# Twelve tiles as 512-column products, and twelve taps of four convolution tiles by ScalarE

## The chip, the cores and the metric

The kernel runs on one core of one Trainium2 chip. The metric is the device time of one execution in microseconds (us). An engine here is one of TensorE (PE; its weight loads are listed as PEld), VectorE (DVE), ScalarE (ACT), GpSimd (POOL) and SyncE (SP). POOL and SP issue transfers (DMA) on queues of their own.

## The reference

One layer of a decoder trunk on 256 rows of width 1024, everything in float32:

```
n = rmsnorm(x);  z = n @ w_in            # one projection, cut into parts
c_a, c_g, q, k, v, qi, ki, wi, gc, ga = split(z)
u = c_a * sigmoid(c_g)                   # convolution branch
u = causal depthwise conv, 31 taps per channel, + bias
y_conv = silu(layernorm(u)) @ w_conv_out
score = sum_h wi_h * relu(qi_h . ki)     # index: 8 heads of 64
y_attn = attention of q, k, v over the 64 best-scored keys @ w_attn_out
h = x + (sigmoid(gc) * y_conv + sigmoid(ga) * y_attn) @ w_mix_out
h = h + cross_attention(rmsnorm(h), rmsnorm(mem))
h = h + relu(rmsnorm(h) @ w_ff1)^2 @ w_ff2
out = rmsnorm(h)
```

The convolution is `u'[t] = bias + sum over s of w[30 - s] * u[t - s]`, s = 0 to 30, for each of the 1024 channels. Channels lie on partitions, so there are eight tiles of 128 channels by 256 rows, and a tap is one multiply-add with a scalar per partition.

## The kernel before

Each float32 product is made of three products of a cheaper form: a number is split into a high part (rounded to fp32r) and a low part (the rest), and high x high, high x low and low x high are added in PSUM. A weight chunk of 1 MB comes by one DMA. For each half of it ACT writes the high part (line 312), and DVE the low part (line 315). PE then makes one product tile of 128 columns of the weight by 256 rows, with eight steps of 128 over the width.

A product tile has two forms (`tile_b`, line 407). The **narrow** form takes 24 matmuls of 256 columns: three for each step (`mm3`). The **wide** form takes the high and the low part of the input side by side as 512 columns, so one matmul of 512 columns makes high x high into the left half of the bank and high x low into the right half; eight more matmuls of 256 columns add low x high to the right half. The two halves are added afterwards: `merge` (line 473) copies the right half out with ACT, and DVE adds the left half. `is_wide` (line 439) names the chunks in the wide form. `back` turns the order of the two kinds of matmul around in every second wide tile.

The chunks follow one list (`STREAM`, line 34): conv 0 to 3, index queries qi, index key ki, conv 4 to 7, the two gates gc and ga, v, then q and k in turns, cross-attention keys and values xk and xv, attention-out ao, conv-out co, mix, and so on to the two feed-forward products f1 and f2. A conv chunk `i` (`conv_in`, line 673) gives two product tiles, gate and value; ACT takes the sigmoid of the gate, DVE multiplies, and the result is `u` for conv tile `i`.

Engines take their instructions in the order in which the program writes them. Between product tiles `tick` (line 369) writes a *turn*: one step of each open chain (generators: memory norm, index scores, gates, attention heads, layer norm), then taps. The taps are what fills DVE: every conv tile has a queue of closures (`tap`, line 628), and `fill_one` (line 378) takes one as long as a running estimate of DVE's time lies behind one of PE's by 1000 ns.

Some taps go another way. Conv tiles 2 to 7 form pairs 1, 2 and 3. From time to time (list `added`, line 352, 25 entries with pauses in estimated PE time) `add_tap` (line 649) lets ACT multiply one shift of both tiles of a pair into a buffer `products`, and POOL issues a DMA that adds it to `acc` in place (line 659). The DVE queue of such a pair is held back until its last DMA has had time (`held_back`). The shifts that go this way are 25 down to 1, in the order of `added`. DVE so has 30 taps for tiles 0 and 1, 25 for 2 and 3, 23 for 4 and 5, 17 for 6 and 7.

When a tile has its last tap, its sum goes into `usum`; with the eighth tile the layer norm starts (`layer_norm`, line 811). It needs the mean (`ps_mub`), the variance (`ps_vr`, `ps_rsb`), and waits until all attention heads are through before it applies the result; its output is the input of conv-out. It gives one step a turn. The heads (line 854) also give one step a turn; the last makes the product `ps_o` and splits it at once.

Of the kernel before, what the change touches and what calls it, by code (L numbers as in the profile page):

```python
# [16 lines left out]
P = 128  # L17
D = 1024
S = 256
# [36 lines left out]
N_CHUNK = KT * S  # L56
HALVES = 6
EARLY = (3,)
WHOLE = (("conv", 0),)
SEVEN = tuple(range(1, 14))  # L60
JOINED = 14
# [57 lines left out]
def block_kernel(ctx, tc, x, xt, mem, memt, wst, wki, vecs, convw, gout, out):  # L119
# [30 lines left out]
    def ps_mm(name):  # L150
        return bank("mm", 2, name)
# [194 lines left out]
        return [w if kt is None else w.rearrange("p (k n) -> p k n", k=kt) for w in prepared.pop(key)]  # L346


    chains, fill, turn, done = [], [], [0], []


    added = [(1, 5000)] * 5 + [(2, 5000)] * 2 + [(2, 2500), (3, 3000)] * 5 + [(3, 5000)] * 8 + []
    add_next, ready, held_back = [0.0], {}, []

    def add_some():
# [13 lines left out]
    def tick():  # L369
        for c in list(chains):  # L370
            if next(c, "end") == "end":
                chains.remove(c)
        while (len(fill) > 1 or (fill and (len(done) > 5 or nused[0] < 5))) and dve.total < pe.total - 1000:
            fill_one()
        dve.total = max(dve.total, pe.total - 2000)
        add_some()

    def fill_one():

        some = [q for q in fill[:3] if q is not turn[0]] or fill  # L380
        q = some[0] if len(some[0]) < 10 and len(fill) > 3 else max(some, key=len)
        turn[0] = q
        q.pop(0)()
        if not q:
            fill.remove(q)
# [5 lines left out]
    def start(gen):  # L391
        chains.append(gen)
        return gen

    def split(hi, lo, src):
        act(hi, src, AF.Copy)
        dve.tensor_tensor(out=lo, in0=src, in1=hi.bitcast(F32), op=ALU.subtract)
# [40 lines left out]

    def is_wide(kind, ct):

        return kind in ("f1", "gc", "ga", "ao", "xk", "q", "k") or (kind in ("mix", "co") and ct < 6)

    def form_b(kind, i, x2, after, ps_of=ps_mm):

# [46 lines left out]
    def copy_to(dst):  # L491
        return lambda ct, ps: copy_out(dst[:, ct, :], ps)
# [135 lines left out]
    def tap(t, s):  # L628
        def go():
            j = TAPS - 1 - s  # L630
            if s == 0:
                act(acc[:, t, :], u[:, t, :], AF.Identity, scale=cw[:, t, j : j + 1], bias=cvb[:, t : t + 1])
            else:
                dve.scalar_tensor_tensor(out=acc[:, t, s:], in0=u[:, t, : S - s], scalar=cw[:, t, j : j + 1],
                                         in1=acc[:, t, s:], op0=ALU.mult, op1=ALU.add)
            if s == TAPS - 1:
                done.append(t)
                if len(done) == KT:
                    norms.append(start(layer_norm()))
                if len(done) > 1:  # L640
                    dve.tensor_tensor(out=usum, in0=usum if len(done) > 2 else acc[:, done[0], :],
                                            in1=acc[:, t, :], op=ALU.add)
        return go

    queues, delays, products = {}, {}, []
    for n, (p, _) in enumerate(added):
        delays.setdefault(p, []).append(len(added) - n)

    def add_tap(pair, s):
        if not products:  # L650
# [10 lines left out]
    def conv_tile(i, half):  # L661
        key = ("conv", i)
        w = weights("conv", i, half, KT) if key not in WHOLE else None
        split_ahead()
        ps = ps_mm(f"ps_conv{i}{half}")
        if w:
            tile_b(ps, w, n2)
        else:
            for kt in range(KT):
                pe.matmul(ps[:, :S], whole[key][:, half * KT + kt, :], n_f[:, kt, :], start=kt == 0, stop=kt == KT - 1)  # L670
        return ps

    def conv_in(i):
        psg = conv_tile(i, 0)
        sg = w2(f"sg{i}", F32, (P, S))
        act(sg, psg[:, :S], AF.Sigmoid)
        tick()
        psa = conv_tile(i, 1)
        dve.tensor_tensor(out=u[:, i, :], in0=psa[:, :S], in1=sg, op=ALU.mult)
        tick()  # L680
        tap(i, 0)()
        queue = [tap(i, s) for s in range(1, TAPS) if s not in delays.get(i // 2, ())]
        if i // 2 not in delays:
            fill.append(queue)
        else:
            queues.setdefault(i // 2, []).append(queue)
            if i % 2:
                delay = iter(delays[i // 2])
                ready[i // 2] = lambda: add_tap(i // 2, next(delay))
        if ("conv", i) in WHOLE:  # L690
            load()
# [6 lines left out]

    qi_t = t8("qi_t", F32, (P, 4, S))
    for i in range(2):  # L700
        form_b("qi", i, n2, copy_to(qi_t))
    wk = weights("ki", 0, 0, KT)
    split_ahead()
    ps = ps_mm("ps_ki")
# [62 lines left out]
    start(index_scores())  # L767
    for i in range(4, 8):
        conv_in(i)


    gc_t, ga_t = t8("gc_t"), t8("ga_t")
# [38 lines left out]
    def layer_norm():  # L811
        u2.append(parts_t8("u_p"))
        mub = ps_aux("ps_mub")[:, :S]
        pe.matmul(mub, onesd, usum, start=True, stop=True)
        mub = mub.unsqueeze(1).to_broadcast([P, 2, S])
        vs = w2("vs", F32, (P, 2, S))
        pairs = [slice(2 * c, 2 * c + 2) for c in range(4)]
        for c, cs in enumerate(pairs):
            dve.tensor_tensor(out=acc[:, cs, :], in0=acc[:, cs, :], in1=mub, op=ALU.subtract)
            sq = vs if c == 0 else w2(f"sq_vr{c}", F32, (P, 2, S))  # L820
            act(sq, acc[:, cs, :], AF.Square)
            if c > 1:
                dve.tensor_tensor(out=vs, in0=vs, in1=before, op=ALU.add)
            before = sq
        yield
        dve.tensor_tensor(out=vs, in0=vs, in1=before, op=ALU.add)
        dve.tensor_tensor(out=vs[:, 0, :], in0=vs[:, 0, :], in1=vs[:, 1, :], op=ALU.add)
        yield
        yield
        rs = rsqrt(vs[:, 0, :], "vr")  # L830
        yield
        while len(headed) < NH:
            yield
        act(table, table, AF.Silu)
        rsb = spread(rs, "rsb").unsqueeze(1).to_broadcast([P, 2, S])
        for c in range(5):
            if c < 4:
                dve.tensor_tensor(out=acc[:, pairs[c], :], in0=acc[:, pairs[c], :], in1=rsb, op=ALU.mult)
                for t in (2 * c, 2 * c + 1):
                    act(acc[:, t, :], acc[:, t, :], AF.Silu, scale=lng[:, t : t + 1], bias=lnb[:, t : t + 1])  # L840
                act(u2[0].high(2 * c, 2), acc[:, pairs[c], :], AF.Copy)
            if c > 0:
                parts_of(2 * c - 2)
            yield
# [9 lines left out]
    def head(h, q, k):  # L854
        yield
        yield
        ps = ps_acc(f"ps_s{h}")
        pe.matmul(ps[:, 0:P], q[:, 0:P], k[:, 0:P], start=True, stop=True)
        pe.matmul(ps[:, P : 3 * P], q[:, P:S], k, start=True, stop=True)
        t = w2(f"att_t{h}", F32, (P, 3 * P))  # L860
        yield
        mx = small.tile([P, 2], F32, tag="mx", name=f"mx{h}")
        sm = small.tile([P, 2], F32, tag="sm", name=f"sm{h}")
        for qb in range(2):
            dve.tensor_tensor_reduce(out=t[:, parts[qb]], in0=ps[:, parts[qb]], in1=bias[qb], scale=1.0,
                                     scalar=-3.0e38, op0=ALU.add, op1=ALU.max, accum_out=mx[:, qb : qb + 1])
        dve.tensor_scalar(mx, mx, -ATT_SCALE, None, ALU.mult)
        yield
        p = w2(f"att_p{h}", F32, (P, 3 * P))
        for qb in range(2):  # L870
            act(p[:, parts[qb]], t[:, parts[qb]], AF.Exp, bias=mx[:, qb : qb + 1], scale=ATT_SCALE,
                accum_out=sm[:, qb : qb + 1])
        yield
        dve.reciprocal(sm, sm)
        yield
        for qb in range(2):
            act(p[:, parts[qb]], p[:, parts[qb]], AF.Copy, scale=sm[:, qb : qb + 1])
        yield
        pt = ps_aux(f"ps_pt{h}")
        for j in range(3):  # L880
            pe.transpose(pt[:, j * P : j * P + P], p[:, j * P : j * P + P], ident)
        ptr = w2(f"ptr{h}", F32, (P, 3 * P))
        act(ptr, pt[:, : 3 * P], AF.Copy)
        yield
        po = ps_aux(f"ps_o{h}")
        hs = slice(h * HD, h * HD + HD)
        pe.matmul(po[:, 0:P], v_rm[:, 0, hs], ptr[:, 0:P], start=True, stop=True)
        pe.matmul(po[:, P:S], v_rm[:, 0, hs], ptr[:, P : 2 * P], start=True, stop=False)
        pe.matmul(po[:, P:S], v_rm[:, 1, hs], ptr[:, 2 * P : 3 * P], start=False, stop=True)
        split(o2.high(h), o2.low(h), po[:, :S])  # L890
        headed.append(h)

# [31 lines left out]
    for i in range(4):  # L924
        form_b("ao", i, o2, lambda ct, ps: start(gate_branch(ct, ps)), ps_turn)
    assert not added and not held_back
    while fill:
        fill_one()
    finish(norms[0])
# [626 lines left out]
```

## Time and profile before

| | us |
|---|---|
| median of 3 runs | 498.96 |
| lowest, highest | 498.74, 499.46 |
| profiled execution | 499.24 |
| its span | 497.5 |
| DVE taps in `acc` (x190), busy | 78.1 |
| ACT products of `add_tap` (x50), busy | 21.9 |
| ACT high parts (x133), busy | 138.6 |
| DVE low parts (x133), busy | 161.2 |

The span is that of the instructions in one profiled execution. Busy times of instructions that overlap on an engine count the overlap in each, so the distance between two starts tells more of what one costs than its own duration. The name of a tile stands without its number: `ps_conv` is any conv product tile. Line 84 is the line of the helper through which all PE and DVE instructions pass.

### The profile page before, as it was taken

How to read it: one execution, taken by the hardware profiler on the slowest of the kernel's cores; microseconds unless marked ns; L12 is line 12 of the kernel's file. 1: busy time of each engine (PE TensorE's matmuls, PEld its weight loads, DVE VectorE, ACT ScalarE, POOL GpSimd, SP SyncE). 2: the span in 40 equal slices, each digit the busy share in tenths (PEclk: the TensorE clock that was granted, in tenths of full speed). 3: DMA queues.
4: the chain of work that ended last, by engine and by line, in shares of the span. 5: the costliest groups of instructions: out<-in, count | busy, mean ns of one | idle time of the engine just before them, and what ended most of it. 6: DMA issues, size and time to landing. Idle time of an engine off the chain costs nothing.

```text
span 497.5 us, 8036 instructions
## 1 busy us (share of the span) xinstructions
PE 488.3 (98%) x2976; PEld 436.0 (88%) x2976; DVE 462.4 (93%) x847; ACT 358.3 (72%) x615; POOL 47.2 (9%) x64
## 2 busy tenths in 40 slices
PE   7999999999999999999999999999999999999995
PEld 5999998888888898888889999988998888888884
DVE  5999899999899889999988987899999999999986
ACT  7657787787756667667946658687777878888852
POOL 2002212111112100000000000000010101130000
PEclk9999999999999999999999999999999999999998
DMA  8958678989788753444644552766979878999802
GB/s 317 377 198 263 187 188 256 244 236 263 233 232 241 200 155 119 164 170 169 243 180 170 195 206 108 267 199 143 250 261 299 244 242 265 270 342 322 260 3 85
DMA packets 31848, 108.99 MB, mean 219 GB/s; under 512 B 11056, under 2 KB 11824, under 8 KB 22848
## 3 DMA queue, kind: packets, MB, share of 16 engines
q1 hardware_dynamic: 24416, 93.03, 54.2%
q0 software_dynamic: 7104, 15.24, 15.6%
q8 instruction: 23, 0.38, 0.3%
q10 hardware_dynamic: 288, 0.20, 0.1%
q14 instruction: 17, 0.14, 0.1%
HBM read 99.29 MB, written 1.05 MB: 202 GB/s over the span
## 4 chain that ended last, share of the span: by engine, by line
PE 92%; DVE 3%; DMA 3%; ACT 1%; issue 0%; POOL 0%; DVEq 0%; SPq 0%; POOLq 0%
PE ps_f L84 16%; PE ps_p L84 13%; PE ps_conv L84 10%; PE ps_co L84 5%; PE ps_mix L84 5%; PE ps_ao L84 5%; PE ps_k L84 4%; PE ps_gc L84 4%; PE ps_ga L84 4%; PE ps_q L84 4%; PE ps_v L84 4%; PE ps_xo L84 3%; PE ps_qi L84 2%; PE ps_xq L84 2%; PE ps_xk L84 2%; PE ps_xv L84 2%
## 5 line engine op out<-in xcount | busy, mean ns | idle before, releaser
L84 DVE TENSOR_TENSOR lo<-raw,hi 128x1024 fp32r<-128x1024 f32 x133 | 161.2, 1215 | 2.5 <-ACT hi L312 2.2
L312 ACT ACTIVATE hi<-raw 128x1024 fp32r<-128x1024 f32 x133 | 138.6, 1048 | 4.6 <-DMA raw<-in_wst_dram 4.5
L84 DVE SCALAR_TENSOR_TENSOR acc<-u,cw,acc 128x234 f32<-128x234 f32 (+29 forms) x190 | 78.1, 463 | 1.5 <-DMA acc<-products 1.2
L84 PE MATMUL ps_f<-ff_p,hi 128*128 128x512 f32 (+1 forms) x320 | 72.5, 348 | 0.1
L84 PEld LDWEIGHTS ps_f<-ff_p,hi 128*128 128x128 f32 x320 | 56.2, 189 | 8.5 <-ACT ft L1268 0.5
L84 PE MATMUL ps_f<-ff_p,lo 128*128 128x256 f32 x256 | 46.8, 282 | 0.0
L84 PE MATMUL ps_conv<-n_p,hi 128*128 128x256 f32 x224 | 41.0, 285 | 0.0
L84 PEld LDWEIGHTS ps_f<-ff_p,lo 128*128 128x128 f32 x256 | 39.3, 190 | 1.8
L84 PEld LDWEIGHTS ps_conv<-n_p,hi 128*128 128x128 f32 x224 | 34.8, 190 | 0.8 <-issue 0.7
L659 POOL DMA_DIRECT2D acc<-products x25 | 21.7, 867 | 125.5 <-ACT products L658 41.3
L84 PE MATMUL ps_conv<-n_p,lo 128*128 128x256 f32 x112 | 31.7, 283 | 0.0
L658 ACT ACTIVATE products<-u,cw 128x231 f32<-128x231 f32 (+24 forms) x50 | 21.9, 489 | 0.0
L84 PEld LDWEIGHTS ps_conv<-n_p,lo 128*128 128x128 f32 x112 | 21.3, 190 | 0.0
L290 ACT ACTIVATE inner<-sums 128x1024 fp32r<-128x1024 f32 x13 | 13.8, 1060 | 10.4 <-DVE sums L84 10.4
L84 DVE TENSOR_TENSOR ft<-ft 128x128 f32<-128x128 f32 (+2 forms) x49 | 19.4, 396 | 1.2 <-ACT ft L1268 0.7
L84 PE MATMUL ps_p<-outer,fs 128*128 128x512 f32 x78 | 20.1, 393 | 0.0
L84 PE MATMUL ps_v<-hi,n_p 128*128 128x512 f32 x64 | 19.9, 389 | 0.0
L84 PE MATMUL ps_p<-inner,fs 128*128 128x512 f32 x78 | 19.8, 389 | 0.0
L84 PE MATMUL ps_co<-u_p,hi 128*128 128x512 f32 (+1 forms) x80 | 19.3, 350 | 0.0
L84 PE MATMUL ps_mix<-mix_p,hi 128*128 128x512 f32 (+1 forms) x80 | 19.2, 349 | 0.0
L84 PE MATMUL ps_k<-n_p,hi 128*128 128x512 f32 x64 | 17.4, 403 | 0.0
L84 PE MATMUL ps_q<-n_p,hi 128*128 128x512 f32 x64 | 17.3, 402 | 0.0
(431 smaller groups left out, 1180.6 us busy)
## 6 DMA issues: line engine op xcount, KB each, us to landing
raw<-in_wst_dram SPq DMA_DIRECT2D x67, 1024.0 KB, 5.6
raw<-in_wst_dram SPq DMA_DIRECT2D x28, 512.0 KB, 6.0
sums<-in_wst_dram POOLq DMA_DIRECT2D x15, 512.0 KB, 7.6
acc<-products POOLq DMA_DIRECT2D x25, 256.0 KB, 6.7
x_rm<-in_x_dram SPq DMA_DIRECT2D x2, 512.0 KB, 4.1
mem_rm<-in_mem_dram SPq DMA_DIRECT2D x1, 1024.0 KB, 8.9
mem_t<-in_memt_dram SPq DMA_DIRECT2D x1, 1024.0 KB, 10.8
h_t<-in_xt_dram SPq DMA_DIRECT2D x1, 1024.0 KB, 7.1
```

Source lines behind the costliest of these rows:

```text
L84: return fn(*args, **kwargs)
L290: act(hi, src, AF.Copy)
L312: act(hi, raw[:, ns], AF.Copy)
L658: act(prod[:, a, s:], u[:, t, : S - s], AF.Copy, scale=cw[:, t, TAPS - 1 - s : TAPS - s])
L659: nc.gpsimd.dma_start(acc[:, ts, :], prod, accum_op=ALU.add)
```

## The change

- Index queries (`qi`, four tiles) and conv chunks 4 to 7 (eight tiles) take the wide form, and take their PSUM banks from two sets in turns (`ps_turn`). The gate tile of such a conv chunk is merged before its sigmoid, the value tile before the product with the gate.
- Conv tiles 4 to 7 give their twelve largest shifts, 19 to 30, to a new chain `four_tiles`, which starts after conv 7. ACT writes each shift of the four tiles into half of a buffer `ring` (the first into `sums`), five instructions in four turns. DVE adds a finished shift of all four tiles to `sums` in one instruction, for shifts 20 to 27; for the last three, 28 to 30, a DMA with addition does it. Four turns later, and once `added` is worked off, DVE adds `sums` to `acc`.
- The chain gives its step at the end of a turn, behind the taps.
- The shifts of `added` are dealt anew: 20 to 16 for pair 1, 15 and 14 and 13 to 9 for pair 2, 13 to 1 for pair 3. DVE is left with 30, 25, 11 and 5 taps for each tile of pairs 0 to 3.
- A tile's taps ended (`last_tap`) and its sum complete (`settled`) are now two events.
- A head, the last one excepted, splits its product one turn later.

```diff
+QUADS = 12
+BY_DMA = 3
+PACE = 5
-    added = [(1, 5000)] * 5 + [(2, 5000)] * 2 + [(2, 2500), (3, 3000)] * 5 + [(3, 5000)] * 8 + []
+    added = [(1, 5000)] * 5 + [(2, 5000)] * 2 + [(2, 2500), (3, 3000)] * 5 + [(3, 5000)] * 8
+    shifts = [*range(20, 13, -1), *(s for s in range(13, 8, -1) for _ in range(2)), *range(8, 0, -1)]
...
-        while (len(fill) > 1 or (fill and (len(done) > 5 or nused[0] < 5))) and dve.total < pe.total - 1000:
+        while (len(fill) > 1 or (fill and (len(ended) > 5 or nused[0] < 5))) and dve.total < pe.total - 1000:
             fill_one()
+        if fours and next(fours[0], "end") == "end":
+            fours.clear()
...
-        return kind in ("f1", "gc", "ga", "ao", "xk", "q", "k") or (kind in ("mix", "co") and ct < 6)
+        return kind in ("f1", "qi", "gc", "ga", "ao", "xk", "q", "k") or (kind in ("mix", "co") and ct < 6)
...
+    def last_tap(t):
+        def go():
+            ended.append(t)
+            if t // 4 not in by_four:
+                settled(t)
+        return go
+
+    by_four = {1: range(31 - QUADS, 31)}
+
+    def four_tiles(g):
+        ts, taps = slice(4 * g, 4 * g + 4), by_four[g]
+        sums = w4(f"four{g}", F32, (P, 4, S))
+        ring = t8(f"ring{g}", F32, (P, 2, 4, S))
+        for n, s in enumerate(taps):
+            dst = ring[:, n % 2, :, s:] if n else sums[:, :, s:]
+            for t in range(4):
+                act(dst[:, t, :], u[:, 4 * g + t, : S - s], AF.Copy, scale=cw[:, 4 * g + t, TAPS - 1 - s : TAPS - s])
+                if (4 * n + t) % PACE != PACE - 1:
+                    yield
+            if 0 < n < QUADS - BY_DMA:
+                dve.tensor_tensor(out=sums[:, :, s:], in0=sums[:, :, s:], in1=dst, op=ALU.add)
+            elif n:
+                nc.gpsimd.dma_start(sums[:, :, s:], dst, accum_op=ALU.add)
+        s = taps[0]
+        for _ in range(4 if BY_DMA else 1):
+            yield
+        while added or held_back:
+            yield
+        dve.tensor_tensor(out=acc[:, ts, s:], in0=acc[:, ts, s:], in1=sums[:, :, s:], op=ALU.add)
+        del by_four[g]
+        for t in ended:
+            if t // 4 == g:
+                settled(t)
...
-        ps = ps_mm(f"ps_conv{i}{half}")
+        ps = (ps_turn if i > 3 else ps_mm)(f"ps_conv{i}{half}")
         if w:
-            tile_b(ps, w, n2)
+            tile_b(ps, w, n2, wide=i > 3, back=back[0])
+            back[0] = i > 3 and not back[0]
...
-        act(sg, psg[:, :S], AF.Sigmoid)
+        if i > 3:
+            merge_now(sg, psg)
+            act(sg, sg, AF.Sigmoid)
+        else:
+            act(sg, psg[:, :S], AF.Sigmoid)
         tick()
         psa = conv_tile(i, 1)
-        dve.tensor_tensor(out=u[:, i, :], in0=psa[:, :S], in1=sg, op=ALU.mult)
+        if i > 3:
+            merge_now(u[:, i, :], psa)
+        dve.tensor_tensor(out=u[:, i, :], in0=u[:, i, :] if i > 3 else psa[:, :S], in1=sg, op=ALU.mult)
         tick()
         tap(i, 0)()
-        queue = [tap(i, s) for s in range(1, TAPS) if s not in delays.get(i // 2, ())]
+        queue = [tap(i, s) for s in range(1, TAPS) if s not in (*delays.get(i // 2, ()), *by_four.get(i // 4, ()))]
+        queue.append(last_tap(i))
...
-        form_b("qi", i, n2, copy_to(qi_t))
+        form_b("qi", i, n2, copy_to(qi_t), ps_turn)
...
     for i in range(4, 8):
         conv_in(i)
+    fours.append(four_tiles(1))
...
         pe.matmul(po[:, P:S], v_rm[:, 1, hs], ptr[:, 2 * P : 3 * P], start=False, stop=True)
+        if h < NH - 1:
+            yield
         split(o2.high(h), o2.low(h), po[:, :S])
...
+    while fours:
+        tick()
     while fill:
         fill_one()
```

More of the change, by code (lines that the diff above doesn't have):

```diff
@@ L346, in weights @@
         return [w if kt is None else w.rearrange("p (k n) -> p k n", k=kt) for w in prepared.pop(key)]
-    chains, fill, turn, done = [], [], [0], []
-    added = [(1, 5000)] * 5 + [(2, 5000)] * 2 + [(2, 2500), (3, 3000)] * 5 + [(3, 5000)] * 8 + []
+    chains, fours, fill, turn, done, ended = [], [], [], [0], [], []
+    added = [(1, 5000)] * 5 + [(2, 5000)] * 2 + [(2, 2500), (3, 3000)] * 5 + [(3, 5000)] * 8
+    shifts = [*range(20, 13, -1), *(s for s in range(13, 8, -1) for _ in range(2)), *range(8, 0, -1)]
     add_next, ready, held_back = [0.0], {}, []
@@ L635, in go, with settled @@
                                          in1=acc[:, t, s:], op0=ALU.mult, op1=ALU.add)
[L636 to L642, printed above, removed]
-        return go
+        return go
+    def settled(t):
+        done.append(t)
+        if len(done) == KT:
+            norms.append(start(layer_norm()))
+        if len(done) > 1:
+            dve.tensor_tensor(out=usum, in0=usum if len(done) > 2 else acc[:, done[0], :],
+                              in1=acc[:, t, :], op=ALU.add)
+    def last_tap(t):
[29 more added lines that the diff above has]
+                settled(t)
     queues, delays, products = {}, {}, []
-    for n, (p, _) in enumerate(added):
-        delays.setdefault(p, []).append(len(added) - n)
+    for s, (p, _) in zip(shifts, added, strict=True):
+        delays.setdefault(p, []).append(s)
     def add_tap(pair, s):
```

## The prediction

> **What bounds the kernel now.** I read the page first: engine totals, slices, the chain that ended last. Then the windows by stage, the chain in order of time, and the timelines of single engines.
>
> ```profile
> span 497.5 us, 8036 instructions
> PE 488.3 (98%) x2976; PEld 436.0 (88%) x2976; DVE 462.4 (93%) x847; ACT 358.3 (72%) x615; POOL 47.2 (9%) x64
> PEclk9999999999999999999999999999999999999998
> PE 92%; DVE 3%; DMA 3%; ACT 1%; issue 0%; POOL 0%; DVEq 0%; SPq 0%; POOLq 0%
> ```
>
> TensorE (PE) is busy 98% of the span at full granted clock, and the last chain is PE for 92%. A busy PE is not yet PE at its best, so the windows must say whether anything else holds it. Their columns are the stretch in us, its length, then busy us of PE, PEld, DVE, ACT and POOL, the clock, DMA share and GB/s:
>
> ```profile
> 47.85:60.83 12.98, 12.98 (x117) 12.57 (x115) 11.37 (x26) 10.95 (x21) 2.15 (x3) 1.00 0.69 181
> 60.83:74.86 14.03, 14.03 (x113) 13.15 (x114) 13.75 (x36) 10.39 (x19) 2.51 (x3) 1.00 0.79 206
> 74.86:97.20 22.34, 22.34 (x130) 19.70 (x129) 21.93 (x56) 16.46 (x30) 4.85 (x7) 1.00 0.86 241
> 97.20:119.50 22.30, 22.30 (x129) 19.69 (x129) 22.30 (x44) 18.51 (x36) 4.62 (x5) 1.00 0.91 256
> 119.50:141.20 21.70, 21.70 (x97) 17.96 (x97) 20.43 (x38) 15.34 (x24) 3.45 (x4) 1.00 0.80 235
> 141.20:166.00 24.80, 24.80 (x143) 21.87 (x142) 24.07 (x55) 16.72 (x34) 3.45 (x4) 1.00 0.85 242
> 166.00:193.00 27.00, 27.00 (x170) 24.21 (x170) 23.36 (x65) 17.34 (x42) 1.72 (x2) 1.00 0.52 151
> ```
>
> In these stretches, conv chunk 4 to the last key chunk, PE is busy for the whole length of each. VectorE (DVE) is full too, but PE never waits for it. So time taken off DVE alone is worth nothing here; only a shorter stream of matmuls is, provided the other engines keep up.
>
> **The matmul stream.** These are pieces of the chain in order of time (start, length, what, matmuls), then the timeline of PE:
>
> ```profile
> 33.30 8.64 PE ps_qi L84 x72
> 61.90 5.95 PE ps_conv L84 x48
> 74.86 22.32 PE ps_gc L84 x128
> ...
> 74.70 2.00 PE L84 MATMUL ps_gc<-n_p,hi 128*128 128x512 f32 x8
> 76.54 1.11 PE L84 MATMUL ps_gc<-n_p,lo 128*128 128x256 f32 x8
> 77.49 0.40 PE L84 MATMUL ps_gc<-n_p,hi 128*128 128x512 f32 x1
> ```
>
> A narrow tile is 24 matmuls of 256 columns: 8.64 / 3 = 2.88 us, 120 ns each. A wide tile is 8 of 512 and 8 of 256: 22.32 / 8 = 2.79 us. The starts in its timeline give (76.54 - 74.70) / 8 = 230 ns and (77.49 - 76.54) / 8 = 119 ns. Columns streamed are the same, 6144; only 2 x 120 - 230 = 10 ns a merged pair is saved. The change turns 4 index tiles and 8 conv tiles wide: 12 x (2.88 - 2.79) = **1.1 us less on PE**. The conv piece gives 5.95 / 2 = 2.98 a tile, but it includes the hand-over to the small fp32 index products, which stays. Taking it as the upper bound gives 4 x 0.09 + 8 x 0.19 = 1.9 us; the lower bound is nothing, should the stream stop for something else. I take 1.1, since two rows of pure tiles give it.
>
> The Trainium skill (TensorE: Matmul & The Clock Gate, Back-to-back issue gap) puts a warm matmul at N / 2.4 + 2.5 ns. By that, leaving out 96 matmuls saves 96 x 2.5 ns = 0.24 us. The trace disagrees: 256 columns take 120 ns, not 109, and 512 take 230, not 216.
>
> **What is added to ScalarE (ACT) and DVE.** Issue distances are read from starts, since instructions overlap:
>
> ```profile
> 80.50 0.39 ACT L475 ACTIVATE gc_t<-ps_gc 128x256 f32<-128x256 f32 x1 [1.47 <-PE ps_gc L84]
> 80.78 0.87 ACT L658 ACTIVATE products<-u,cw 128x238 f32<-128x238 f32 x2
> 81.55 1.05 ACT L312 ACTIVATE hi<-raw 128x1024 fp32r<-128x1024 f32 x1
> 82.50 0.50 ACT L780 ACTIVATE gc_t<-gc_t,vec 128x256 f32<-128x256 f32 x1
> ...
> 206.04 0.42 DVE L84 TENSOR_TENSOR kv<-ps_xk,kv 128x256 f32<-128x256 f32 x1
> 206.37 1.56 DVE L84 SCALAR_TENSOR_TENSOR acc<-u,cw,acc 128x232 f32<-128x232 f32 x4
> 207.85 1.22 DVE L84 TENSOR_TENSOR lo<-raw,hi 128x1024 fp32r<-128x1024 f32 x1
> 208.99 0.42 DVE L84 TENSOR_TENSOR o_p<-ps_o,o_p 128x256 fp32r<-128x256 f32 x1
> ```
>
> ACT: a copy out of PSUM 0.28 us, a tap product 0.77 / 2 = 0.385, a high part 0.95. DVE: a merge 0.33, a tap 1.48 / 4 = 0.37, a low part 1.14.
>
> DVE loses 12 x 4 = 48 taps x 0.37 = 17.8 us. It gains 8 adds of four tiles and one at the end (about 920 columns, estimated from the 1024-column low part as 1.0 us each: 9.2), and 12 merges x 0.33 = 4.0. Net 4.6 us less. DVE is not what ends the path, so this is costed at nothing.
>
> ACT gains 8 copies x 0.28 = 2.2 us in the conv stage (the index queries were copied by ACT before too) and 48 x 0.385 = 18.5 us of tap products. With PACE 5 there are five products in four turns, one turn being one product tile. Product 47 falls in turn 39, and turns 1 to 40 are the gc, ga, v, q and k tiles, 74.9 to about 193 us. ACT's idle time there, from the windows, is 5.9 + 3.8 + 6.4 + 8.1 + 9.7 = 33.9 us. So 18.5 fit; the tight stage is ga, with 10 products (3.9 us) into 3.8 us. I cost them at nothing while ACT may run a few us late. Its allowance is this count of low parts made when PE reaches the first gate tile:
>
> ```profile
> L84 DVE TENSOR_TENSOR lo<-raw,hi x22: 750/1217/1222, 13.2 to 74.1; 128x1024 fp32r<-128x1024 f32 x21, 128x576 fp32r<-128x576 f32 x1
> ACT acc L632 <- DVE u L84: 8.2, 6, 2.9
> ACT o_p L396 <- PE ps_o L84: 9.1, 7, 1.7
> ```
>
> Nineteen of the 22 served conv 1 to 7, qi and ki; three tiles, 3 x 2.79 = 8.4 us, lie ready. The other two rows are from the waits (total us, times, longest). The change adds waits in the conv chunks: ACT's sigmoid now waits for DVE's merge, and behind it stand the next high part and copies. The row nearest to it is ACT waiting for u, 8.2 / 6 = 1.4 us; bounds are 0.3 (a merge alone) and 2.6 (two low parts and a merge first). I take 1.4. The `yield` before a head's split goes the other way: ACT no longer waits 9.1 us for the head's product, which frees ACT but no PE time.
>
> Banks: conv tiles now alternate between two sets, so each is free later but reused later; I see no wait of PE there and cost it at nothing. The merges hide behind the next tiles' matmuls; a merge that PE waited for would cost its 0.33 us. The new list of shifts moves the 25 earlier product pairs to other taps, and the fill's test now counts tiles whose own taps have ended; neither changes how much work an engine gets.
>
> **The three transfers and the end.** First the products' transfers (KB each, median us to landing) and the last one of before, then the layer norm's products:
>
> ```profile
> acc<-products POOLq DMA_DIRECT2D x25, 256.0 KB, 6.7
> sums<-in_wst_dram POOLq DMA_DIRECT2D x15, 512.0 KB, 7.6
> 172.50 0.86 POOL L659 DMA_DIRECT2D acc<-products  x1 [5.26 <-ACT att_p L877]
> ...
> 221.27 0.43 PE ps_mub L84 x2
> 233.31 0.22 PE ps_rsb L84 x2
> 244.69 22.57 PE ps_co L84 x144
> ```
>
> The three new transfers (about 465 KB) are issued in turns 33, 37 and 40, 9 us or more apart, at about 7 us each; the ring's second half is written again four turns after its transfer left. They pass in POOL's queue only the last product transfers. The final add comes in turn 44 (about 208 us), after the pair-3 queue (5 taps a tile instead of 17) has run out. The layer norm then starts in turn 45. Now it starts in turn 48 (221.27) and gives its last low part as conv-out begins (244.69) without PE waiting. So it has three turns, 8 us, to spare: no gain, and no loss unless the add slips by more than that. Beyond it each late turn would show as a PE gap of some 2 us before 244.7.
>
> Sum: -1.1 on PE, 0 elsewhere. The profiled execution took 499.24 us (span 497.5 and 1.7 around it), which gives 498.1. It lies 0.3 above the median of the runs, 498.96; against that the forecast is **497.9 us**.
>
> **The rivals.**
> - *ACT falls too far behind (slower).* From 47.85 to 119.5 us ACT has 2.0 + 3.6 + 5.9 + 3.8 = 15.3 us idle. It must take copies 2.2, 20 products 7.7 and 8 new waits. At 1.4 us a wait that is 21.1, a lag of 5.8 us, under the 8.4 that lie ready. PE stalls from 1.7 us a wait on, and the kernel is slower than before from 1.9. At 2.3 (two low parts stand ahead of the merge) the lag is 13.0, PE loses 4.6, net +3.5: 502.5 us. For it: DVE is full in these windows. Against: ACT waits before nearly every gate copy now (1.47 in the row). The Trainium skill (ScalarE: Activation LUTs, Rules for kernel authors) says to multiply and add on VectorE rather than ScalarE; the rows make it 0.385 against 0.37 us a tap, so the rule alone decides nothing. Chance 0.17.
> - *Only part arrives.* Merges and late copies cost PE a few tenths of us at the seams, for instance two gaps the size of a merge: 1.1 - 0.66 = 0.4 us, 498.5. Against: banks enough for four tiles. Chance 0.12.
> - *The stream does not shorten by merging.* A matmul's fixed part is small, and the wide tile is faster only as its low products are, 119 against 120 ns: 12 x 24 x 1 ns = 0.3 us, 498.7. Against: 230 ns for 512 columns. Chance 0.03. The Trainium skill's 2.5 ns, above, would come to nearly this time.
> - *More arrives.* The conv tiles really run at 2.98 and become 2.79: 1.9 us, 497.1. Against: the distances inside a tile are 120 ns. Chance 0.05.
>
> **How the numbers follow.** The forecast has 0.63, with its own range 497.4 to 498.5. A change of 0.2% (1.0 us, about what a measurement of this kernel can tell from none) lies at 497.96, just above it, so I give 0.42 of the 0.63 to faster and 0.21 to the same. With the rivals: faster 0.42 + 0.05 = 0.47, same 0.21 + 0.12 + 0.03 = 0.36, slower 0.17. The range reaches from 497.1 to 499.7, into the mild end of the first rival (waits of about 2.0 us); its harder end is left out.
>
> **What would show it.** Right: ps_qi and ps_conv pieces at 2.79 a tile, all PE stages after 75 us moved forward by about 1.1 us, DVE's busy time lower by about 5 us, ACT's up by about 20. Wrong: idle PE with a high part or a merge as releaser between 50 and 125 us (first rival), a gap before the first ps_co matmul (late layer norm), or wide conv tiles still at 2.88.

## The result, and the profile after

| | before | changed |
|---|---|---|
| median of 13 runs, us | 498.83 | 501.62 |
| lowest, highest | 498.73, 504.88 | 500.50, 507.02 |
| ratio (95% interval) | | 1.006 (1.0034 to 1.0087) |
| profiled execution, span | 499.24, 497.5 | 504.95, 503.1 |

The change makes the kernel 0.6% slower, 2.8 us; 497.9 had been forecast, in a range that ended at 499.7. Of the 13 executions ten took 500.5 to 502.2 us and three 505 to 507, and the profiled one is of the upper group, so a second one, of 501.13 us (a2 below), is read beside it. The ratios, here and below, average over the executions and leave out those that lie more than 1.5% above the fastest of the same kernel (one of f1, two of h2, one of the kernel before), so they need not follow the medians.

The page of the changed kernel: the totals, and the slices of PE (40 of 12.6 us, busy share in tenths).

```profile
span 503.1 us, 7878 instructions
PE 488.3 (97%) x2880; PEld 430.7 (86%) x2880; DVE 458.2 (91%) x820; ACT 375.7 (75%) x671; POOL 52.6 (10%) x67
PE   7999999999999997989999999999999999999995
```

The row of PE before the change (slices of 12.4 us):

```profile
PE   7999999999999999999999999999999999999995
```

DVE has 4.2 us less to do and ACT 17.4 more. PE has 96 matmuls fewer. But there is a dent in PE's row in the slices from about 188 to 226 us, where it had none. The chain in order of time (start, length, what, matmuls) shows where the 1.1 us are won and where they are lost:

```profile
33.17 8.36 PE ps_qi L87 x48
67.95 5.80 PE ps_conv L87 x32
73.75 22.29 PE ps_gc L87 x128
...
140.09 5.57 PE ps_q L87 x32
...
230.72 0.22 PE ps_rsb L87 x2
...
250.46 22.57 PE ps_co L87 x144
```

| start of | before | changed | changed, usual (a2) |
|---|---|---|---|
| first gate tile | 74.86 | 73.75 | 73.80 |
| first q tile | 141.23 | 140.09 | 140.14 |
| first conv-out tile | 244.69 | 250.46 | 246.25 |
| span | 497.5 | 503.1 | 499.3 |

Up to the first q tile PE is 1.1 us ahead, as forecast, and it stays busy throughout. Between q and conv-out a usual execution loses 2.7 us against before, this one 6.9. Behind conv-out nothing more changes. The windows (columns as before) and the waits of PE (total us, times, longest), 150 to 260 us; before the change PE waits for nothing in that stretch:

```profile
165.00:192.00 27.00, 23.82 (x149) 21.18 (x148) 20.95 (x56) 16.14 (x40) 4.33 (x4) 1.00 0.67 168
192.00:220.00 28.00, 26.72 (x155) 23.10 (x155) 26.27 (x66) 19.44 (x50) 1.28 (x1) 1.00 0.66 182
220.00:244.00 24.00, 22.66 (x132) 19.60 (x131) 19.52 (x31) 21.01 (x37) 1.61 (x1) 1.00 0.40 137
```

```profile
PE ps_o L87 <- ACT ptr L936: 3.7, 2, 3.2
PE ps_mub L87 <- DVE usum L87: 1.3, 1, 1.3
PE ps_vr L87 <- DVE o_p L87: 0.8, 1, 0.8
```

Two different things stand there. The 3.2 us end with ACT, so the question is what held ACT. These are its timeline and then POOL's, where `four<-ring` are the new transfers and `acc<-products` the old ones:

```profile
181.27 0.39 ACT L481 ACTIVATE q<-ps_q 128x256 f32<-128x256 f32 x1
189.15 0.86 ACT L671 ACTIVATE ring<-u,cw 128x226 f32<-128x226 f32 x2 [7.50 <-DMA four<-ring]
189.91 1.04 ACT L315 ACTIVATE hi<-raw 128x1024 fp32r<-128x1024 f32 x1
190.86 0.47 ACT L936 ACTIVATE ptr<-ps_pt 128x384 f32<-128x384 f32 x1
```

```profile
171.62 0.86 POOL L703 DMA_DIRECT2D acc<-products  x1 [7.86 <-ACT att_p L930]
179.42 0.86 POOL L703 DMA_DIRECT2D acc<-products  x1 [6.94 <-DVE acc L87]
179.96 1.66 POOL L677 DMA_DIRECT2D four<-ring  x1
189.66 1.28 POOL L677 DMA_DIRECT2D four<-ring  x1 [8.05 <-DMA four<-ring]
```

The last product transfer waits 6.9 us, until 179.42; the first ring transfer stands behind it in POOL's queue and lands only at 189.1. ACT comes at 181.7 to write the same ring half again, waits 7.5 us, and behind it stand the next high part and the head's `ptr`, for which PE waits. In the usual execution (a2) the same transfer goes out at 168.2 and no such wait exists:

```profile
167.68 0.86 POOL L703 DMA_DIRECT2D acc<-products  x1 [3.49 <-ACT ring L671]
168.22 1.66 POOL L677 DMA_DIRECT2D four<-ring  x1
```

What is left in the usual execution are three short waits of PE; these are its rows, 30 to 300 us, and then DVE's timeline around the final add:

```profile
PE ps_vr L87 <- DVE o_p L87: 0.8, 1, 0.8
PE ps_o L87 <- ACT ptr L936: 0.5, 1, 0.5
PE ps_mub L87 <- DVE usum L87: 0.5, 1, 0.5
```

```profile
207.42 1.14 DVE L87 TENSOR_TENSOR acc<-acc,four 128x948 f32<-128x948 f32 x1
208.60 1.81 DVE L87 TENSOR_TENSOR usum<-usum,acc 128x256 f32<-128x256 f32 x4
210.32 1.22 DVE L87 TENSOR_TENSOR lo<-raw,hi 128x1024 fp32r<-128x1024 f32 x1
...
212.18 1.87 DVE L87 TENSOR_TENSOR acc<-acc,ps_mub 128x512 f32<-128x512 f32 x3
```

The add, four sums that depend on one another, and the layer norm's subtractions stand in one lump on DVE, in the turns in which the last heads need DVE and ACT for their scores. PE, also in order, has the mean's product `ps_mub` queued ahead of the next tiles and waits for the last of the sums. The waits add to 1.8 us, and behind each the next piece of the chain is some 0.27 us longer (`ps_vr` 0.61 us in a2 against 0.34 before); together that is about the 2.7 us lost. The longest of the three, at `ps_vr`, ends not with the norm's work but with a head's split (`o_p`).

### The profile page after: what moved, and what is told of

Its sections match the earlier page's. It is cut to its first block, busy times and chain, and to the rows that moved or that the text cites. A ratio compares the mean times of both kernels' runs of the same rounds, so it can differ in the third digit from the quotient of the medians.

```text
span 503.1 us, 7878 instructions
## 1 busy us (share of the span) xinstructions
PE 488.3 (97%) x2880; PEld 430.7 (86%) x2880; DVE 458.2 (91%) x820; ACT 375.7 (75%) x671; POOL 52.6 (10%) x67
## 4 chain that ended last, share of the span: by engine, by line
PE 89%; DMA 4%; DVE 3%; ACT 2%; issue 1%; POOL 0%; DVEq 0%; SPq 0%; POOLq 0%
PE ps_f L87 18%; PE ps_p L87 15%; PE ps_conv L87 9%; PE ps_co L87 4%; PE ps_mix L87 4%; PE ps_ao L87 4%; PE ps_gc L87 4%; PE ps_ga L87 4%; PE ps_v L87 4%; PE ps_q L87 3%; PE ps_xo L87 3%; PE ps_k L87 3%; PE ps_xq L87 2%; PE ps_qi L87 2%; DMA four<-ring 2%; PE ps_xk L87 2%
## 5 line engine op out<-in xcount | busy, mean ns | idle before, releaser
L87 DVE SCALAR_TENSOR_TENSOR acc<-u,cw,acc 128x255 f32<-128x255 f32 (+27 forms) x142 | 58.7, 466 | 0.3
L87 PE MATMUL ps_conv<-n_p,hi 128*128 128x256 f32 (+1 forms) x160 | 34.3, 330 | 0.0
L87 PEld LDWEIGHTS ps_conv<-n_p,hi 128*128 128x128 f32 x160 | 26.6, 190 | 2.8 <-issue 0.7
L671 ACT ACTIVATE ring<-u,cw 128x236 f32<-128x236 f32 (+10 forms) x44 | 20.2, 481 | 7.5 <-DMA four<-ring 7.5
L87 PE MATMUL ps_conv<-n_p,lo 128*128 128x256 f32 x112 | 22.5, 283 | 0.0
L702 ACT ACTIVATE products<-u,cw 128x243 f32<-128x243 f32 (+19 forms) x50 | 22.1, 493 | 0.0
L87 PEld LDWEIGHTS ps_conv<-n_p,lo 128*128 128x128 f32 x112 | 18.0, 191 | 0.5
L87 PE MATMUL ps_k<-n_p,hi 128*128 128x512 f32 x64 | 17.4, 404 | 0.0
```

The source lines that it names most:

```text
L87: return fn(*args, **kwargs)
L671: act(dst[:, t, :], u[:, 4 * g + t, : S - s], AF.Copy, scale=cw[:, 4 * g + t, TAPS - 1 - s : TAPS - s])
L702: act(prod[:, a, s:], u[:, t, : S - s], AF.Copy, scale=cw[:, t, TAPS - 1 - s : TAPS - s])
```

## The experiments

Two theories were put up. **A**: ACT waits for a ring transfer that is late in POOL's queue. **B**: the layer norm's start in turn 45, and the lump of work in front of it, collide with the last heads. A third, **C**, was the recorded rival: ACT has too much to do. All ratios are against the kernel before, run beside each of them. e2, e3 and e4 have four executions each, a2 one, the others ten.

**The parts of the change alone.**

```diff
-BY_DMA = 3
+BY_DMA = 0          # e1
+BY_DMA = 2          # e2
```

e1: 

> The last three taps of the four tiles are added by VectorE too (BY_DMA = 0), so no transfer stands between ScalarE and the ring. Theory A (ScalarE waits for the first ring transfer, which is late behind the product adds in POOL's queue): no wait of ScalarE on a ring transfer, no gap of PE between 170 and 192 us, about 498 to 499 us, at most the 2.6 us of gaps after 192 left. Theory B (the layer norm's earlier start collides with the last heads): the start comes no later than in the changed kernel, gaps of PE of 2 to 3 us between 195 and 244 us stay, about 500 us. Theory C (ScalarE has simply too much to do): 501 us or more, gaps from 75 us on.

e2: 

> Only the last two taps of the four tiles go by transfer (BY_DMA = 2), so neither ring half is written again after its transfer. Theory A: ScalarE no longer waits for a transfer; 498 to 499 us. Theory B: unchanged, 500 us or more, with gaps of PE between 195 and 244 us. Theory C: unchanged, about 501.6 us.

```diff
-    fours.append(four_tiles(1))                        # e3: wide tiles (and the heads' later splits)
-    by_four = {1: range(31 - QUADS, 31)}
+    by_four = {}
-    shifts = [*range(20, 13, -1), ...]
+    shifts = [*range(25, 0, -1)]
```

e3: 

> Wide tiles and the heads' later split alone; the taps as before the change. Theories A and B both put the loss on the taps' new way, so this should show the bare gain: 1.1 us less than before, 497.7 us, if VectorE keeps up with 12 more merges; with the taps left on VectorE (4 us more for it before the layer norm) it may start the norm one or two turns late and lose 1 to 3 us at conv-out. Theory C: 497.7 us.

```diff
-    return kind in ("f1", "qi", "gc", ...              # e4: taps (and the heads' later splits)
+    return kind in ("f1", "gc", ...
-    (ps_turn if i > 3 else ps_mm), wide=i > 3, ...
+    ps_mm, wide=False, ...
```

e4: 

> The four tiles' taps by ScalarE and by transfer, with narrow tiles as before. Theory A and B: the whole loss, 502 to 503 us (the changed kernel plus the 1.1 us of the wide tiles). If the loss comes from the merges in the conv stage, about 499 us.

| | median us | ratio (interval) | first ps_co |
|---|---|---|---|
| e1, no transfer | 499.93 | 1.0016 (1.0007 to 1.0025) | 245.12 |
| e2, two transfers | 501.55 | 1.0049 (1.0033 to 1.0066) | 246.91 |
| e3, wide tiles, no new taps | 505.28 | 1.0131 (1.0116 to 1.0146) | 245.36 |
| e4, taps, narrow tiles | 501.97 | 1.0059 (1.0044 to 1.0074) | 247.24 |

e2 has no reuse of a ring half after a transfer and is as slow as the usual execution of the changed kernel, so A is not what sets the median. e4 has narrow tiles and the same loss from the first q tile to conv-out, 2.6 us: it comes with the taps or with the later splits, which all four keep. e1 was a surprise. Its norm did not start early: with three more adds on DVE the last sums came at 216.4 us and not by 210.4 as in a2, and `ps_mub` at 221.44, in turn 48 as before; one PE wait of 0.8 us is left. PE is busy without a gap up to 193 us in all four, so C falls.

e3 missed by far (497.7, or 1 to 3 us more, was expected), and says how tight DVE was. Its timeline of DVE, then windows of PE (stretch, length, busy, clock, DMA share, GB/s):

```profile
221.25 1.54 DVE L87 SCALAR_TENSOR_TENSOR acc<-u,cw,acc 128x227 f32<-128x227 f32 x4
222.71 1.22 DVE L87 TENSOR_TENSOR lo<-raw,hi 128x1024 fp32r<-128x1024 f32 x1
223.84 0.81 DVE L87 SCALAR_TENSOR_TENSOR acc<-u,cw,acc 128x226 f32<-128x226 f32 x2
...
227.30 0.42 DVE L87 TENSOR_TENSOR usum<-usum,acc 128x256 f32<-128x256 f32 x1
```

```profile
240.00:245.00 5.00, 3.66 (x24) 1.00 0.81 306
245.00:250.00 5.00, 3.29 (x10) 0.82 0.62 262
250.00:255.00 5.00, 4.86 (x15) 0.50 0.26 72
```

With twelve merges more, 3.8 us of DVE's busy time, the last sum comes at 227.3 instead of 220.0 before: only a part of a turn is left for taps. (The later splits are in e3 too; what they add to this was not separated.) The norm is late for conv-out: PE begins it at 245.36, 0.7 us after the kernel before, has five gaps, 3.1 us in all, ahead of and among its first pieces between 240 and 250, and then streams at a granted clock of 0.50 for about five us.

**The norm in its old turn.** In f1 the four sums are completed one a turn, 44 to 47:

```diff
-        for t in ended:
-            if t // 4 == g:
-                settled(t)
+        for n, t in enumerate([t for t in ended if t // 4 == g]):
+            if n:
+                yield
+            settled(t)
```

f2 is f1 with `BY_DMA = 2`; f2b is f2 with `if h < NH - 2` in place of `NH - 1`, so head 6 splits its product at once; f3b is f2b with `BY_DMA = 0`. These and all later runs that keep the taps also keep the pause of four turns ahead of the final add when nothing goes by transfer, where e1 pauses for one.

f1: 

> The changed kernel with its four sums completed in four turns instead of one (turns 44 to 47), so that the layer norm takes its first step in turn 48, as before the change. Theory B (the norm's early start: add, four dependent sums and the mean's product stand in one lump ahead of the last heads on VectorE, and PE waits for the mean's product): the median falls by about 2 us to 499 to 499.5. Theory A (the ring's transfers): the median stays near 501.6. If both hold, most executions near 499 and a few of 503 to 505, where ScalarE waits for a ring half.

f2: 

> As f1, and only the last two taps by transfer, so no ring half is written again after its transfer. Theory B: 498.5 to 499, with the one remaining PE wait of 0.8 us at the mean's product, which waits for a bank that head 6 leaves only in turn 48. Theory A: like f1 without its slow executions. If neither holds: 501.5, as with two transfers and the lump.

f2b: 

> As f2, and head 6 splits its product at once, as before the change, so its bank is free a turn earlier. Theory B with the bank: no PE wait at ps_mub, 0.8 us less than f2: 497.8 to 498.2, below the kernel before.

f3b: 

> As f2b without any transfer (two more adds of 1.1 us on VectorE). If VectorE has time to spare before the layer norm: the same as f2b. If it is at its limit, as the run with wide tiles alone says: the last taps come late and the time is 1 to 2 us above f2b.

| | median us | ratio (interval) | first ps_co |
|---|---|---|---|
| f1 | 500.71 | 1.0051 (1.0016 to 1.0086) | 244.75 |
| f2 | 499.62 | 1.0014 (1.0005 to 1.0023) | 244.93 |
| f2b | 498.97 | 0.9999 (0.9988 to 1.0010) | 243.62 |
| f3b | 498.85 | 0.9990 (0.9979 to 1.0002) | 243.69 |

Against e2, f2 differs in the spread sums alone, and the ratio falls by 0.0035, 1.7 us: theory B. The edit breaks up the lump and moves the norm's start at once; which of the two counts for how much it doesn't say. Between f2 and f2b the ratio falls by 0.0015, 0.7 us; the intervals just overlap, but the only PE wait of f2 goes:

```profile
PE ps_mub L87 <- DVE o_p L87: 0.8, 1, 0.8
```

The mean's product takes the bank that head 6 leaves, and the later split leaves it in the same turn. In a2 and e2 a wait for `o_p` of the same length stands at `ps_vr`, which leaves the other two rows, 1.0 us in a2 and 1.5 in e2, to the norm's early start; that the bank is the reason there too is read from the releaser, and no run moves head 6's split with the norm early. The profiled execution of f2b has no PE wait from 30 to 260 us and reaches conv-out at 243.62, 1.07 us before the old kernel. That execution took 498.39 us; the ten spread from 498.0 to 500.0, and what the longer ones lose was not traced, so the median is that of the kernel before. f2 and f2b came 0.6 and 0.8 us above what had been expected of them. The DVE timeline of f2b shows the same work without the lump:

```profile
207.94 1.15 DVE L87 TENSOR_TENSOR acc<-acc,four 128x948 f32<-128x948 f32 x1
209.12 0.42 DVE L87 TENSOR_TENSOR usum<-usum,acc 128x256 f32<-128x256 f32 x1
...
211.33 0.41 DVE L87 TENSOR_TENSOR usum<-usum,acc 128x256 f32<-128x256 f32 x1
...
212.79 0.42 DVE L87 TENSOR_TENSOR usum<-usum,acc 128x256 f32<-128x256 f32 x1
...
217.27 0.41 DVE L87 TENSOR_TENSOR usum<-usum,acc 128x256 f32<-128x256 f32 x1
```

f3b disproves its pessimistic branch: with the sums spread, two more adds cost nothing. f1 did worse than expected; four of its ten executions lie above 503 us, none of f2's, which fits theory A, though the intervals overlap.

**What is left.**

```diff
+            if n == QUADS - 1:                         # g1, from f1 with NH - 2
+                last = t8(f"last{g}", F32, (P, 4, S))
...
-        if h < NH - 2:                                 # g3, from f2b
-            yield
...
-        queue = [tap(i, s) for s in range(1, TAPS) ... # g2, from e3 (with the changed kernel's list of shifts)
+        queue = [tap(i, s) for s in range(1, TAPS - 12 * (i > 3)) ...
```

h1 is g3 with the loop over `taps` and the final add taken out of `four_tiles`, and 43 turns of nothing in their place. h2 and h3 are g3 with `BY_DMA` 3 and 0. g2 and h1 leave the twelve taps of conv tiles 4 to 7 out altogether: they don't compute the layer, and show only what the rest costs.

g1: 

> Three transfers as in the changed kernel, the sums spread and head 6 as before the change, and a buffer of its own for the last tap, so that ScalarE never writes a ring half after its transfer (the buffer is that of the product adds, free once the last of them has landed). Theory A: the slow executions of 503 to 507 us, seen in the changed kernel and in f1, go or shrink; median 498 to 499. If the number of transfers and not the reuse of the half makes them: some executions above 503 stay.

g2: 

> Wide tiles alone, as in e3, and the twelve taps of conv tiles 4 to 7 left out altogether (the convolution lacks them), so VectorE has 17.8 us less to do before the layer norm. If e3 lost its 6 us because VectorE's taps ended late: 497.5 to 498, the bare gain of the wide tiles. If the wide conv tiles themselves cost (merges, banks): 500 us or more.

g3: 

> As f2b, with no head's split moved. Theory: only head 6's bank mattered, so the time is that of f2b, 498 to 499; ScalarE waits about 9 us more for the heads' products, hidden. If the later splits are needed to relieve ScalarE: 1 us or more above f2b, with PE waits for ScalarE between 175 and 220 us.

a2: 

> The changed kernel once more, for a trace of a usual execution (500.5 to 502.2 us in ten of its 13 runs). Theories A and B together: no wait of ScalarE for a ring half, and PE waits at ps_mub, ps_vr and ps_o of some 2.5 us between 195 and 245 us. If it falls among the executions above 503 us: the wait for the ring half again.

h1: 

> Wide tiles, the twelve taps of conv tiles 4 to 7 left out altogether as in g2, but the sums held so that the layer norm takes its first step in turn 48; no head's split moved. If g2 lost its 3.5 us to the norm's early start alone: 497.6 to 498.0, and PE reaches the first conv-out product 1.1 us before the kernel before (243.6 against 244.7). If the wide conv tiles cost something later: 499 or more. If executions above 503 us come from the early start, none here.

h2: 

> As g3 (no head's split moved, sums spread), with three transfers instead of two, so that ScalarE writes one ring half again four turns after its transfer was put in POOL's queue. Theory A: most executions at 498 to 498.5 like g3, and some of 503 or more, in which ScalarE waits for the ring half. If the reuse is harmless: none above 500.

h3: 

> As g3 without transfers: two more adds of 1.1 us on VectorE. Expected the same as g3, 498.1, since f3b and f2b agree; 1 us more if VectorE's taps then end after turn 47.

| | median us | lowest, highest | ratio (interval) |
|---|---|---|---|
| g1 | 498.54 | 497.90, 503.00 | 1.0003 (0.9984 to 1.0022) |
| g2 | 501.31 | 500.29, 507.74 | 1.0062 (1.0028 to 1.0096) |
| g3 | 498.10 | 497.67, 498.85 | 0.9983 (0.9973 to 0.9993) |
| h1 | 498.07 | 497.75, 505.07 | 0.9998 (0.9970 to 1.0026) |
| h2 | 498.82 | 498.06, 506.25 | 0.9993 (0.9983 to 1.0003) |
| h3 | 498.20 | 497.68, 500.94 | 0.9989 (0.9975 to 1.0003) |

g2 has 17.4 us less on DVE than e3 (448.8 against 466.2) and is slow all the same, where 497.5 to 498 had been expected if DVE's late taps were all that e3 lost by. The waits of PE in g2 (30 to 260 us; h1 has none), then its chain, and that of h1, which differs in the norm's turn (and in the heads' splits):

```profile
PE ps_o L87 <- DVE acc L87: 0.7, 1, 0.7
PE ps_mub L87 <- ACT ptr L935: 0.6, 1, 0.6
PE ps_s L87 <- DVE k L87: 0.3, 1, 0.3
```

```profile
189.81 0.71 PE ps_mub L87 x2
...
226.26 0.22 PE ps_rsb L87 x2
246.00 22.57 PE ps_co L87 x144
```

```profile
220.35 0.43 PE ps_mub L87 x2
...
243.77 22.57 PE ps_co L87 x144
```

With its taps done early, g2 starts the norm at 189.8, among the heads; the norm's result must wait for the last head anyway (`ps_rsb` at 226), so nothing is won, and conv-out begins at 246.0. Held back to turn 48 it begins at 243.8. This is theory B without any of the new taps and without the final add; the later splits of g2 may have a part in it, at the bank of `ps_mub`. g1 and h2 against g3 say less about theory A than hoped: their intervals overlap. The profiled execution of h2, a long one with a span of 504.4 us, does show ACT waiting 8.25 us for a ring half:

```profile
190.49 0.86 ACT L671 ACTIVATE ring<-u,cw 128x226 f32<-128x226 f32 x2 [8.25 <-DMA four<-ring]
```

Counted over all runs, 9 of 38 executions took 503 us or more where a ring half is written again behind one of three transfers (the changed kernel, a2, e4, f1, h2), none of 64 with the same taps and two transfers or none, and 1 of 10 in g1, which has three transfers and no such reuse. That speaks for theory A as one cause of long executions. It isn't the only one: 4 of 20 come in g2 and h1, which have no ring, and 2 of 107 in the kernel before. What the others are was not settled.

g3 is faster than both kernels: 0.17% below before (0.07 to 0.27%), 0.9 us of the median. Its profiled execution, 498.85 us and the longest of its ten, reaches conv-out 1.07 us early and loses 0.7 of that again behind it.

## Why the prediction was wrong

- **The wide tiles**: right. 8.36 / 3 = 2.79 us a qi tile, 1.1 us ahead at the first gate tile, and still 1.07 ahead at conv-out in f2b and g3. The 10 ns for each merged pair held, and the 2.5 ns a matmul of the Trainium skill (TensorE: Matmul & The Clock Gate, Back-to-back issue gap), which gives them for the isolated gap, did not.
- **ACT** (the first rival, 0.17): the kernel came out slower, as this rival had it, but not by its mechanism. PE has no gap between 30 and 165 us in any run; the merges and 48 products were absorbed. DVE's saving, 4.2 us against 4.6 worked out, was right too.
- **"It has three turns, 8 us, to spare: no gain, and no loss unless the add slips by more than that"**: this step failed. I counted the turns to the deadline and took early work for free. I did not ask beside whose work it would then stand: engines work in order, so the norm's lump (3 us on DVE, a product on PE that waits for it) now stands ahead of the last heads. That is 1.7 us (e2 to f2), and g2 against h1 shows 2.2 us at conv-out without the new taps, the splits included. The forecast named the start in turn 45 and the waits of the heads' chain, but did not put them in one row.
- **The banks, "I see no wait of PE there"**: I looked at the conv tiles' banks only. The later split of head 6 keeps a bank that the norm's products need: 0.7 us (f2 to f2b), the `ps_mub` row in f2 and, by its releaser, the `ps_vr` row in a2.
- **The transfers "pass in POOL's queue only the last product transfers"**: true, and mis-sized. I took 7 us each from issue to landing; the first ring transfer took 9.2 (changed kernel) and 12.1 (a2), and the last product transfer itself waits up to 7 us before it is issued, so the first ring transfer goes out at 168 to 180 us and the four turns until its half is written again are not always enough. It lengthened the profiled execution by 4 us against a2, and that of h2, where the clock fell too, by 7 against g3; its share of the median was not separated from noise.
- **"Time taken off DVE alone is worth nothing here"**: not contradicted (e4 took 8 us off DVE and was no faster), but the other side of it was left out. DVE's taps end just in time, and 4 us more on it cost 6.5 (e3, later splits included). In these runs the wide tiles pay only together with relief for DVE; I costed the one without saying that it depends on the other.

## What to carry to other kernels

When an edit makes a step ready earlier, place it: list what stands behind it on each in-order engine in the new turn, because starting early before a result that must wait anyway only delays others. If an engine is full but off the path, find the last thing it must deliver, since that deadline is where added work turns up, larger than it is. Before a buffer is written again behind a queued transfer, count the waits of everything ahead of that transfer in its queue, not its own length.

## What the runs showed of the hardware

After gaps of PE the granted clock fell in two traces. In e3 five gaps of 1.71, 0.49, 0.34, 0.29 and 0.23 us between 243.6 and 249.5 us were followed by five us at 0.50 (the windows above). In h2 a wait of 4.3 us, up to 192.7 us, was followed by matmuls at 0.65 to 0.67:

```profile
190.00:195.00 5.00, 2.28 (x10) 0.67 0.50 66
195.00:200.00 5.00, 5.00 (x24) 0.65 0.93 254
```

In the changed kernel the 3.2 us wait left the clock at 1.00. Where the clock fell, the gaps cost about twice their length: from the first q tile to conv-out h2 took 110.7 us against 103.5 in g3, 7.2 us for a wait of 4.3, and from the first q tile to the end of the span e3 took 363.3 against 356.3 before, 7.0 us for gaps of 3.1. The Trainium skill (TensorE: Matmul & The Clock Gate, Part 1) has the clock halve after an idle window of about 3.4 us that runs freely. The 0.50 agrees, but e3's gaps were each shorter than the window; a free-running window might explain why a gap sometimes costs and sometimes not, which no run here shows.

Four sums that depend on one another cost DVE 0.46 us each from start to start (four in 1.81 us, a2); an addition of the same width that waits for none before it (`kv`, among the rows of the prediction) cost 0.33.
